# A hybrid encoder layer whose inputs also arrive transposed, with the norm weights applied in the operands' split and the tokens' factors applied to results

## The chip, the cores and the metric

The kernel runs on one core of a Trainium2 chip. A core has a matrix engine (TensorE, called PE in the profile; PEld is its weight load), a vector engine (VectorE, DVE), an engine for functions of one operand (ScalarE, ACT), a general one (GpSimd, POOL) and SyncE (SP), which here only issues DMAs. Each works through its own list of instructions in a fixed order, and waits at an instruction until what it needs has been written. The metric is device time in microseconds of one execution.

## The reference, cut to what matters

One layer over 1024 tokens of 1024 channels (x) and 256 tokens of a memory (mem). Both are normalised first, and everything before the attention is computed from the two normalised arrays:

```python
def rmsnorm(x, w):                      # each token by its own mean square, each channel by w
    return x * rsqrt(mean(x * x, axis=-1) + EPS) * w

mem_n = rmsnorm(mem, norm_mem_w)        # 256 x 1024
kv    = mem_n @ xkv_w                   # 256 x 2048, used later by the cross-attention

hn    = rmsnorm(x, norm_mix_w)          # 1024 x 1024
ca, cb, rq, rk, rv, rg = split(hn @ w_in)        # 512, 512, 256, 256, 512, 512 columns
u     = ca * sigmoid(cb)                # causal depthwise convolution, 31 taps, over u
y_conv = silu(layernorm(conv31(u) + conv_b))
q, k  = rotate(rq, positions), rotate(rk, positions)     # angles: position * inv_freq
y_ret = silu(rg) * groupnorm(retention(q, k, rv))        # 8 heads, in chunks
h     = x + concat(y_conv, y_ret) @ w_out
# then h += cross-attention to kv, h += squared-ReLU MLP, and a last rmsnorm
```

## The kernel before, in words

Large products are made from operands split in two: `hi` is the value rounded to the type fp32r, `lo` the rest. `mm3` issues three products, hi·hi (L128), hi·lo (L129) and lo·hi (L130). A split of what has been loaded is a copy on ACT (L110) and a subtraction on DVE (L111); `load` is a DMA (L120) and a split. Most of the memory on the chip is one pool of 39 slots of 4 KB per partition, given out first in, first out: a DMA into a slot waits until its last reader is done. A framework decides each engine's order of instructions when the program is built; on the chip the order is fixed.

The products need x and mem with channels on the partitions, and the inputs come with tokens there. So the kernel loads 128 tokens at a time (`fetch`, L180), squares and sums a row on ACT (L160), finds the reciprocal root on POOL (`rstd_of`, L142 and L143), multiplies by it and by the norm's weights, broadcast to all partitions (`row`, L148), on DVE (L162), transposes 128x128 blocks on PE against an identity (L170 for x: 64 of them; L203 for the memory: 16) and splits what comes out, from the accumulator memory, on ACT (L174) and DVE (L175, for the memory L208).

The program's first part goes in this order. The memory is prepared; `mem_project` c = 0 to 3 multiplies it by 256 columns of `xkv_w` each, ACT copies the result (L226) and a DMA stores it (`kvT_d`); between these, the eight tiles of x are prepared (`x_load`, `x_prep`). Then come a transpose of the convolution's parameters (L295, into `par`) and one of the positions (L321); DVE copies the latter to `pos_f` (L322). From `pos_f` POOL works out the rotary angles, reduced exactly to one turn, in some 70 small instructions (L328, L330, L333; "the angle chain"), and ACT takes cosine and sine (L379, L380) into `cos_t` and `sin_t`.

`conv_input(m)`, m = 0 to 3, makes 128 channels of u: four groups of 24 products of 512 columns (cb and ca for each half of the tokens), the sigmoid on ACT (L396), the product with ca on DVE (L397). Its weights are loaded one step ahead (L120, `raw`); the other four `mem_project` stand in the program between conv_input(0) and conv_input(1). The convolution is 124 steps on DVE (`conv_steps`, L433, 31 taps for each m; a tap's first one is L430), which the framework places where it thinks that DVE is free. Then V (copied by ACT) and g (Silu on ACT) are made for each tile of 128 tokens, and last the stage of the retention: for each tile a product with the q and k weights, `rotate` on DVE (L478, L483, L485, L488), `turn`, which transposes the rotated tile on PE (L497), and `retain`, with products of its own (L516, L532) and the update of a state on DVE. The weights of the output projection (`w_out`) are loaded while this stage runs, four after its tile 4 and four after tile 5. The cross-attention and the MLP follow.

Of the kernel before, what the change touches and what calls it, by code (L numbers as in the profile page):

```python
# [68 lines left out]
def encoder_layer(ctx: ExitStack, tc: tile.TileContext, x, mem, positions, norm_mix_w, w_in, conv_w, conv_b,  # L69
                  conv_ln_w, conv_ln_b, ret_gn_w, w_out, norm_xattn_w, norm_mem_w, xq_w, xkv_w, xo_w,  # L70
# [5 lines left out]
    memf = mem.rearrange("b s d -> (b s) d")  # L76
# [16 lines left out]
    def tbank():  # L93
        return bank("tp", 3)
# [19 lines left out]
    def load(w, k0, nk, c0, ncol, spare=False):  # L114

        if spare:
            raw = get([P, nk, ncol])
        else:
            raw = stage_tile([P, nk, ncol])
        sync.dma_start(raw[:], w[k0 * P:(k0 + nk) * P, c0:c0 + ncol].rearrange("(k p) c -> p k c", p=P))  # L120
        hi, lo = split(raw, [P, nk, ncol])
        if spare:
            put(raw)
        return hi, lo
# [7 lines left out]

    ident_if = keep.tile([P, C_DM], F32, name="ident_if")
    sync.dma_start(ident_if[:], consts[:, :C_DM])
    ident, invf = ident_if[:, :P], ident_if[:, C_IF:C_DM]
    mhalf = keep.tile([P, 32], F32, name="mhalf")
    vec.memset(mhalf[:], -0.5)
# [39 lines left out]

    def fetch(src):
        t = get([P, D])
        sync.dma_start(t[:], src)  # L180
        return t

    mems = [fetch(memf[t * P:(t + 1) * P, :]) for t in range(2)]
    mrow = row(norm_mem_w)
    mT_hi = [get([P, 2, 512], F32R) for _ in range(2)]
    mT_lo = [get([P, 2, 512], F32R) for _ in range(2)]

    def mem_view(tiles, k):

        return tiles[k // 4].t.rearrange("p a b -> p (a b)")[:, (k % 4) * M:(k % 4 + 1) * M]  # L190

    def mem_weights(c, spare=False):
        return [load(xkv_w, 4 * q, 4, 256 * c, 256, spare) for q in range(2)]

    mw = {0: mem_weights(0)}
    for t in range(2):
        xn = mems[t]
        rms_scaled(xn[:], mrow[:], xn[:])
        for q in range(2):
            tp = tbank()  # L200
            for kk in range(4):
                k = q * 4 + kk
                pe.transpose(tp[:, kk * P:(kk + 1) * P], xn[:, k * P:(k + 1) * P], ident)  # L203
            v = tp[:].rearrange("p (k c) -> p k c", k=4)
            h = mT_hi[q].t.rearrange("p a b -> p (a b)").rearrange("p (k m) -> p k m", k=4)[:, :, t * P:(t + 1) * P]
            l = mT_lo[q].t.rearrange("p a b -> p (a b)").rearrange("p (k m) -> p k m", k=4)[:, :, t * P:(t + 1) * P]
            act.copy(h, v)
            vec.tensor_tensor(out=l, in0=v, in1=f32(h), op=ALU.subtract)  # L208
        put(xn)
    put(mrow)  # L210
# [3 lines left out]
    def mem_project(c):  # L214
# [4 lines left out]
        for j in range(2):  # L219
            o = ps[:, j * M:(j + 1) * M]  # L220
            for k in range(NK):
                hi, lo = w[k // 4]
                lc = slice(j * P, (j + 1) * P)
                mm3(o, hi[:, k % 4, lc], lo[:, k % 4, lc], mem_view(mT_hi, k), mem_view(mT_lo, k),
                    k == 0, k == NK - 1)
        act.copy(st[:], ps[:].rearrange("p (j m) -> p j m", j=2))  # L226
# [5 lines left out]
    xT = [([get([P, 2, 512], F32R) for _ in range(4)], [get([P, 2, 512], F32R) for _ in range(4)]) for _ in range(2)]  # L232
    xs = {}

    def x_load(*ts):
        for t in ts:
            xs[t] = fetch(xf[t * P:(t + 1) * P, :])

    def x_prep(*ts):
        for t in ts:  # L240
            xn = xs.pop(t)
            rms_scaled(xn[:], xrow[:], xn[:])
# [981 lines left out]
```

## Time and profile before

| what | value |
|---|---|
| median of 3 runs | 1310.49 us (1307.62 to 1312.49) |
| the profiled execution's own time | 1311.58 us |
| its span in the trace | 1309.8 us |
| mean granted TensorE clock | 0.993 |
| busy: PE / DVE / ACT / POOL | 1279.6 / 862.3 / 548.4 / 95.7 us |
| the first 60 us: PE / DVE / ACT / POOL | 48.0 / 39.5 / 39.6 / 13.1 us |
| 60 to 120 us | 60.0 / 41.0 / 23.4 / 39.8 us |
| 120 to 260 us | 138.7 / 138.0 / 22.5 / 0.0 us |
| 260 to 420 us | 156.9 / 112.9 / 90.5 / 25.4 us |

The busy time of an engine is the time in which it has an instruction under way; times within the program are microseconds from the span's start. A row of the trace names the start, the duration, the engine, the line of the kernel, what is written and what is read, and in brackets how long the engine had stood idle before it and on whom it waited. A group's row gives the number of instructions, their busy time, the mean duration in ns, and the idle time just before them.

### The profile page before, as it was taken

To read this page: it belongs to the slowest core of one execution; us is meant where nothing else is said; L and a number is where in the kernel's file an instruction comes from. 1 tells how busy PE (TensorE), PEld (TensorE's weight loads), DVE (VectorE), ACT (ScalarE), POOL (GpSimd) and SP (SyncE) were. 2 spreads that over 40 slices of the span, in tenths; PEclk is the share of its full clock that TensorE was granted. 3 is DMA by queue.
4 is the path that set the end of the run, shared out by engine and by line. 5 is a ranking of instruction groups with operands and counts; after the bars stand their busy time and mean duration, and the time that the engine had idled before them with its cause. 6 is when DMAs were issued, how large, how long until landed. Compare 5 with 4: busy or idle time off the path is not lost.

```text
span 1309.8 us, 15796 instructions
## 1 busy us (share of the span) xinstructions
PE 1279.6 (98%) x6093; PEld 1066.4 (81%) x6093; DVE 862.3 (66%) x1090; ACT 548.4 (42%) x1015; POOL 95.7 (7%) x157
## 2 busy tenths in 40 slices
PE   6999999999999999999998999999999999999997
PEld 6898887877888888888877888888888888888886
DVE  6677999977756424574568655555564976577744
ACT  6533112155845323452236554444464344323422
POOL 3192000011211000000000000000000000000002
PEclk9999999999999999999998999999999999999999
DMA  9552103312142401232142443334469544444313
GB/s 340 167 154 89 32 17 97 113 41 89 35 143 93 130 4 41 90 112 72 58 145 81 177 161 145 119 123 177 161 240 400 198 159 152 141 149 159 106 65 129
DMA packets 82100, 166.99 MB, mean 127 GB/s; under 512 B 5310, under 2 KB 42310, under 8 KB 82025
## 3 DMA queue, kind: packets, MB, share of 16 engines
q1 hardware_dynamic: 82024, 165.98, 37.1%
q8 instruction: 48, 0.79, 0.2%
q14 instruction: 28, 0.22, 0.0%
HBM read 119.83 MB, written 46.14 MB: 127 GB/s over the span
## 4 chain that ended last, share of the span: by engine, by line
PE 78%; DVE 13%; POOL 3%; DMA 3%; issue 2%; ACT 1%; SPq 0%; POOLq 0%; ACTq 0%; DVEq 0%
PE mm L130 21%; PE mm L129 21%; PE mm L128 21%; DVE s L433 9%; PE tp L128 3%; PE tp L130 3%; PE tp L129 3%; DVE s L111 2%; POOL s L328 2%; PE mm L516 1%; POOL s L333 1%; PE mm L532 1%; ACT s L110 1%; DMA raw<-in_w_out_dram 1%; DMA s<-in_conv_w_dram 1%
## 5 line engine op out<-in xcount | busy, mean ns | idle before, releaser
L129 PE MATMUL mm<-s,s 128*128 128x512 f32 (+1 forms) x1298 | 494.3, 381 | 3.2 <-DVE s L111 1.7
L128 PE MATMUL mm<-s,s 128*128 128x512 f32 (+1 forms) x1272 | 485.0, 383 | 2.5 <-ACT s L856 1.0
L130 PE MATMUL mm<-s,s 128*128 128x512 f32 (+1 forms) x1222 | 462.0, 381 | 1.1 <-DVE s L111 1.1
L129 PEld LDWEIGHTS mm<-s,s 128*128 128x128 f32 x1298 | 245.3, 189 | 49.0 <-DVE s L111 2.5
L128 PEld LDWEIGHTS mm<-s,s 128*128 128x128 f32 x1272 | 240.4, 189 | 47.8 <-ACT s L856 1.3
L130 PEld LDWEIGHTS mm<-s,s 128*128 128x128 f32 x1222 | 230.9, 189 | 43.8 <-DVE s L111 1.7
L110 ACT CAST s<-s 128x1024 fp32r<-128x1024 f32 x101 | 104.8, 1051 | 143.6 <-DVE s L911 40.9
L433 DVE SCALAR_TENSOR_TENSOR s<-s,par,s 128x1009 f32<-128x1009 f32 (+25 forms) x120 | 146.1, 1276 | 0.5
L111 DVE TENSOR_TENSOR s<-s,s 128x1024 fp32r<-128x1024 f32 x81 | 98.3, 1224 | 57.0 <-ACT s L110 45.5
L111 DVE TENSOR_TENSOR s<-raw,s 128x1024 fp32r<-128x1024 f32 x64 | 78.8, 1237 | 55.1 <-ACT s L110 22.5
L110 ACT CAST s<-raw 128x1024 fp32r<-128x1024 f32 x66 | 69.3, 1055 | 93.2 <-PE mm L129 15.3
L142 POOL TENSOR_SCALAR tiny<-tiny 128x1 f32<-128x1 f32 (+1 forms) x50 | 18.4, 368 | 1177.2 <-ACT junk L160 921.1
L911 DVE TENSOR_TENSOR s<-s,s 128x1024 f32<-128x1024 f32 x38 | 46.0, 1223 | 7.3 <-DMA s<-in_mlp_down_w_dram 5.1
L129 PE MATMUL mm<-s,r 128*128 128x512 f32 x124 | 48.3, 390 | 0.0
L128 PE MATMUL tp<-s,s 128*128 128x512 f32 x120 | 46.8, 390 | 0.0
L110 ACT CAST s<-r 128x1024 fp32r<-128x1024 f32 x26 | 27.2, 1050 | 42.9 <-PE mm L129 13.5
L130 PE MATMUL tp<-s,s 128*128 128x512 f32 x114 | 44.2, 389 | 0.0
L162 DVE SCALAR_TENSOR_TENSOR s<-s,tiny,s 128x1024 f32<-128x1024 f32 x23 | 29.4, 1283 | 20.3 <-POOL tiny L143 12.8
L111 DVE TENSOR_TENSOR s<-r,s 128x1024 fp32r<-128x1024 f32 x22 | 26.9, 1225 | 21.4 <-ACT s L110 15.3
L130 PE MATMUL mm<-s,r 128*128 128x512 f32 x100 | 39.0, 390 | 0.0
L160 ACT ACTIVATE junk<-s 128x1024 f32<-128x1024 f32 x24 | 25.6, 1065 | 31.8 <-DVE s L1115 24.0
L130 PE MATMUL mm<-r,s 128*128 128x512 f32 x98 | 38.1, 389 | 0.0
(273 smaller groups left out, 1857.5 us busy)
## 6 DMA issues: line engine op xcount, KB each, us to landing
s<-in_mlp_down_w_dram SPq DMA_DIRECT2D x24, 512.0 KB, 3.8
s<-in_mlp_up_w_dram SPq DMA_DIRECT2D x23, 512.0 KB, 4.1
aS<-s SPq DMA_DIRECT2D x22, 512.0 KB, 8.5
raw<-in_w_in_dram SPq DMA_DIRECT2D x20, 512.0 KB, 4.2
s<-aS SPq DMA_DIRECT2D x20, 512.0 KB, 3.8
s<-a SPq DMA_DIRECT2D x19, 512.0 KB, 4.6
a<-s SPq DMA_DIRECT2D x18, 512.0 KB, 2.8
raw<-in_xkv_w_dram SPq DMA_DIRECT2D x16, 512.0 KB, 4.4
```

What stands on the lines that cost most here:

```text
L110: act.copy(hi[:], raw[:])
L111: vec.tensor_tensor(out=lo[:], in0=raw[:], in1=f32(hi[:]), op=ALU.subtract)
L128: pe.matmul(ps, lh, rh, start=first, stop=False, skip_group_check=goes_on)
L129: pe.matmul(ps, lh, rl, start=False, stop=False, skip_group_check=goes_on)
L130: pe.matmul(ps, ll, rh, start=False, stop=last, skip_group_check=goes_on)
L142: pool.tensor_scalar(out=v[:], in0=ss, scalar1=scale, scalar2=EPS, op0=ALU.mult, op1=ALU.add)
L160: act.activation(junk[:], src, AF.Square, accum_out=ss[:])
L162: vec.scalar_tensor_tensor(out=dst, in0=src, scalar=rs[:], in1=r, op0=ALU.mult, op1=ALU.mult)
L328: pool.tensor_scalar(out=o, in0=i, scalar1=a, scalar2=None, op0=op0)
L333: pool.tensor_tensor(out=o, in0=a, in1=b, op=op)
L433: vec.scalar_tensor_tensor(out=accs[m][:, s:], in0=us[m][:, :S - s], scalar=cw(m, k), in1=accs[m][:, s:], op0=ALU.mult, op1=ALU.add)
L911: vec.tensor_tensor(out=o[:], in0=a[:], in1=b[:], op=ALU.subtract)
```

## The change

The host passes three more arrays: x transposed (`x_t`), mem transposed (`mem_t`), and the weights of the two norms as columns (`norm_cols`). x itself is still passed, for the residual.

- The 80 transposes, the normalising instruction and the two broadcasts of weights are gone. A row of x_t has one channel on each partition and all tokens along it, so the norm's weight is one number per partition: `scaled_split` makes hi on ACT as a copy with a scale, and lo on DVE as raw · w - hi in one instruction. The operands hold x · w, without the tokens' factors.
- The tokens' factors, 1 / rms, are worked out beside this. ACT squares each raw tile; for x, POOL adds the eight squares up in seven instructions of 128x1024 (L277 of the new kernel); for the memory DVE reduces them. `token_factors` sums over the partitions with products of two columns against ones, ACT copies the sums, POOL finds the reciprocal roots. This gives `x_rs`, tokens on the partitions. `spread` makes the row form: DVE multiplies the identity by a column of factors, PE multiplies ones by that (L224), ACT copies it out: `x_rb` and `mem_rs`, the same on every partition.
- The factors enter where results are read. In `conv_input` DVE multiplies cb by `x_rb` (L440), the sigmoid works in place (L441), DVE multiplies by `x_rb` (L442) and then by ca (L443, as before). In `mem_project` the copy on ACT becomes a multiplication on DVE (L254). V's copy and g's Silu take the factor as the scale of the same ACT instruction. For q and k POOL multiplies `cos_t` and `sin_t` by the factors, two instructions.
- mem_project(3) and the loads around it stand in another order, `mw[4]` is loaded before conv_input(0)'s weights, x's operands are freed only after tile 5 of the retention, and all eight loads of `w_out` stand there.

```diff
+    def scaled_split(hi, lo, raw, w):
+        act.activation(hi, raw, AF.Copy, scale=w)
+        vec.scalar_tensor_tensor(out=lo, in0=raw, scalar=w, in1=f32(hi), op0=ALU.mult, op1=ALU.subtract)
...
+    def token_factors(sums, nt, out):
+
+        ps = tbank()
+        for t in range(nt):
+            for z, q in enumerate(sums):
+                pe.matmul(ps[:, 2 * t:2 * t + 2], q[:, t * P:(t + 1) * P], ones[:, :2], start=z == 0,
+                          stop=z == len(sums) - 1)
+        ss = tiny(nt)
+        act.copy(ss[:], ps[:, :2 * nt].rearrange("p (t z) -> p t z", z=2)[:, :, 0])
+        r = rstd_of(ss[:], 1, 1.0 / D, nt)
+        if out is not None:
+            vec.tensor_copy(out, r[:])
+        return r
+
+    def spread(r, t, ps, scratch):
+
+        vec.tensor_scalar(out=scratch, in0=ident, scalar1=r[:, t:t + 1], scalar2=None, op0=ALU.mult)
+        pe.matmul(ps, ones, scratch, start=True, stop=True)
...
-        act.copy(st[:], ps[:].rearrange("p (j m) -> p j m", j=2))
+        vec.tensor_tensor(out=st[:], in0=ps[:].rearrange("p (j m) -> p j m", j=2),
+                          in1=mem_rs.unsqueeze(1).to_broadcast([P, 2, M]), op=ALU.mult)
...
-    def x_prep(*ts):
-        for t in ts:
-            xn = xs.pop(t)
-            rms_scaled(xn[:], xrow[:], xn[:])
-            transposed(xn, *xT[t // 4], (t % 4) * P)
-            put(xn)
...
+    def x_prep(*ks):
+        for k in ks:
+            raw = xs.pop(k)
+            xT[k] = hi, lo = get([P, S], F32R), get([P, S], F32R)
+            scaled_split(hi[:], lo[:], raw[:], mix_w[:, k:k + 1])
+            sq = get([P, S])
+            act.activation(sq[:], raw[:], AF.Square)
+            if not xss:
+                xss.append(sq)
+            else:
+                pool.tensor_tensor(out=xss[0][:], in0=xss[0][:], in1=sq[:], op=ALU.add)
+                put(sq)
+            put(raw)
...
+    x_rb = get([P, S])
+    token_factors([xss[0][:]], NT, x_rs)
+    for half in range(2):
+        tp = tbank()
+        for i in range(4):
+            spread(x_rs, half * 4 + i, tp[:, i * P:(i + 1) * P], work[:, 5 + i % 3, :])
+        act.copy(x_rb[:, half * 512:(half + 1) * 512], tp[:])
+    put(xss.pop())
...
+            vec.tensor_tensor(out=uh, in0=pb[:], in1=x_rb[:, hh], op=ALU.mult)
+            act.activation(uh, uh, AF.Sigmoid)
+            vec.tensor_tensor(out=uh, in0=uh, in1=x_rb[:, hh], op=ALU.mult)
             vec.tensor_tensor(out=uh, in0=pa[:], in1=uh, op=ALU.mult)
...
-    nxt = conv_weights(0)
-    mw[4] = mem_weights(4)
...
-        if t == 4:
-            wo += [load(w_out, k, 1, 0, D) for k in range(4)]
         if t == 5:
             for w in wqk:
                 put(*w)
-            wo += [load(w_out, k, 1, 0, D) for k in range(4, NK)]
+            for k in range(NK):
+                put(*xT[k])
+            wo += [load(w_out, k, 1, 0, D) for k in range(NK)]
```

How the change moves instructions is seen in the order that each engine is given. In a row stand the line, the operation, what is written and read (tp and mm are accumulators, s_ a slot of the pool, ident_if the identity) and the size.

PE, around the transpose of the positions (tp<-ident_if,s 128x8), before; mm_780 and mm_781 are the accumulators of conv_input(0)'s second half, mm_845 that of a mem_project:

```order
L128 MATMUL mm_781<-s_20_150,s_61_705 128x512
L128 MATMUL mm_780<-s_20_150,s_63_711 128x512
L128 MATMUL mm_845<-s_4_83,s_65_717 128x256
L129 MATMUL mm_845<-s_6_85,s_65_717 128x256
L130 MATMUL mm_845<-s_4_83,s_66_718 128x256
L129 MATMUL mm_781<-s_24_154,s_61_705 128x512
L295 MATMUL tp_630<-ident_if,s_53_623 128x35 x4
L321 MATMUL tp_643<-ident_if,s_55_639 128x8
L130 MATMUL mm_781<-s_20_150,s_62_706 128x512
L128 MATMUL mm_781<-s_20_150,s_61_705 128x512
```

and after, where mm_656 is an accumulator of conv_input(0)'s second half, and mm_723 that of mem_project(4):

```order
L124 MATMUL mm_656<-s_61_454,s_77_597 128x512
L125 MATMUL mm_656<-s_60_453,s_78_598 128x512
L123 MATMUL mm_656<-s_63_460,s_77_597 128x512
L224 MATMUL tp_494<-s_11_114 128x128 x3
L335 MATMUL tp_514<-ident_if,s_67_507 128x35 x4
L361 MATMUL tp_527<-ident_if,s_69_523 128x8
L124 MATMUL mm_656<-s_64_461,s_77_597 128x512
L125 MATMUL mm_656<-s_63_460,s_78_598 128x512
L123 MATMUL mm_723<-s_3_79,s_53_387 128x256
L124 MATMUL mm_723<-s_5_81,s_53_387 128x256
L125 MATMUL mm_723<-s_3_79,s_54_388 128x256
```

Before, the transpose stands in the midst of conv_input(0)'s second half, 45 products ahead of its end; now two products are left there, behind the products that spread the factors (L224).

POOL, from the first instruction that reads data, before (L142 and L143 are the reciprocal roots for a tile of tokens):

```order
L142 TENSOR_SCALAR tiny_101<-tiny_99 128x1
L143 TENSOR_TENSOR tiny_102<-tiny_101,mhalf 128x1
L142 TENSOR_SCALAR tiny_122<-tiny_120 128x1
L143 TENSOR_TENSOR tiny_123<-tiny_122,mhalf 128x1
L142 TENSOR_SCALAR tiny_230<-tiny_228 128x1
L143 TENSOR_TENSOR tiny_231<-tiny_230,mhalf 128x1
```

and after:

```order
L277 TENSOR_TENSOR s_27_224<-s_27_224,s_30_230 128x1024
L138 TENSOR_SCALAR tiny_129<-tiny_127 128x2
L277 TENSOR_TENSOR s_27_224<-s_27_224,s_40_305 128x1024
L139 TENSOR_TENSOR tiny_130<-tiny_129,misc 128x2
L277 TENSOR_TENSOR s_27_224<-s_27_224,s_43_312 128x1024
L277 TENSOR_TENSOR s_27_224<-s_27_224,s_49_375 128x1024
L277 TENSOR_TENSOR s_27_224<-s_27_224,s_52_382 128x1024
L277 TENSOR_TENSOR s_27_224<-s_27_224,s_62_457 128x1024
L277 TENSOR_TENSOR s_27_224<-s_27_224,s_65_464 128x1024
L138 TENSOR_SCALAR tiny_479<-tiny_477 128x8
L139 TENSOR_TENSOR tiny_480<-tiny_479,misc 128x8
L373 TENSOR_TENSOR s_70_530<-pos_f,ident_if 128x128
```

Between the two reciprocal roots for the memory and the one for x now stand the additions, and the angle chain (from L373) follows behind them.

ACT, around the sine (sin_t), before (L226 copies a result of the memory, L396 is conv_input(1)'s sigmoid):

```order
L110 CAST s_90_1090<-raw_1088 128x1024
L110 CAST s_92_1096<-raw_1094 128x1024
L380 ACT_TABLE_LOAD
L380 ACTIVATE sin_t<-s_56_646 128x8x16
L226 COPY s_89_1036<-mm_1037 128x512
L110 CAST s_95_1207<-raw_1205 128x1024
L379 ACTIVATE cos_t<-s_56_646 128x128
L110 CAST s_97_1213<-raw_1211 128x1024
L110 CAST s_101_1431<-raw_1429 128x1024
L396 ACT_TABLE_LOAD
L396 ACTIVATE s_94_1100<-mm_1102 128x512
```

and after (L441 is the sigmoid of conv_input(1), L109 a copy for a split):

```order
L109 CAST s_102_974<-raw_972 128x1024
L109 CAST s_105_1089<-raw_1087 128x1024
L109 CAST s_107_1095<-raw_1093 128x1024
L420 ACT_TABLE_LOAD
L420 ACTIVATE sin_t<-s_70_530 128x8x16
L441 ACT_TABLE_LOAD
L441 ACTIVATE s_104_978<-s_104_978 128x512
L419 ACT_TABLE_LOAD
L419 ACTIVATE cos_t<-s_70_530 128x128
```

Between the sine and the first sigmoid of conv_input(1) stood three copies of weights, a result of the memory and the cosine; now that sigmoid comes right behind it, and the cosine behind the sigmoid.

DVE, at the first rotation (rot, L478), before (L433 is a convolution step, L488 the last instruction of a rotation):

```order
L433 SCALAR_TENSOR_TENSOR s_60_702<-s_100_1322,par,s_60_702 128x997
L433 SCALAR_TENSOR_TENSOR s_60_702<-s_100_1322,par,s_60_702 128x996
L478 TENSOR_TENSOR rot_1969<-mm_1944,cos_t 128x512
L483 TENSOR_TENSOR rb_1970<-mm_1944,sin_t 128x16x16 x2
L433 SCALAR_TENSOR_TENSOR s_60_702<-s_100_1322,par,s_60_702 128x995
L485 TENSOR_TENSOR rot_1969<-rot_1969,rb_1970 128x512
L478 TENSOR_TENSOR rot_2002<-mm_1977,cos_t 128x512
L433 SCALAR_TENSOR_TENSOR s_60_702<-s_100_1322,par,s_60_702 128x994
L488 TENSOR_TENSOR kz_1975<-rot_1969,rconst 128x256
```

and after (L479 is a convolution step, L524 and L529 a rotation's first instructions, L564 the retention's masked scores):

```order
L479 SCALAR_TENSOR_TENSOR s_73_587<-s_109_1099,par,s_73_587 128x996
L479 SCALAR_TENSOR_TENSOR s_74_588<-s_110_1208,par,s_74_588 128x1002
L524 TENSOR_TENSOR rot_1859<-mm_1834,cos_t 128x512
L529 TENSOR_TENSOR rb_1860<-mm_1834,sin_t 128x16x16 x2
L479 SCALAR_TENSOR_TENSOR s_73_587<-s_109_1099,par,s_73_587 128x995
L524 TENSOR_TENSOR rot_1892<-mm_1867,cos_t 128x512
L479 SCALAR_TENSOR_TENSOR s_74_588<-s_110_1208,par,s_74_588 128x1001
L531 TENSOR_TENSOR rot_1859<-rot_1859,rb_1860 128x512
L479 SCALAR_TENSOR_TENSOR s_73_587<-s_109_1099,par,s_73_587 128x994
L479 SCALAR_TENSOR_TENSOR s_74_588<-s_110_1208,par,s_74_588 128x1000
L524 TENSOR_TENSOR rot_1940<-mm_1915,cos_t 128x512
L534 TENSOR_TENSOR kz_1865<-rot_1859,rconst 128x256
```

Before, two steps of the convolution are left at the first rotation; now the steps of two channels' groups (s_73 and s_74) stand between the instructions of the rotations, ten from here on.

168 lines of the change are left out of this document (87 added, 81 removed).

## The prediction

> **What bounds the kernel now.** I read the page's first part, the waits of TensorE, the busy times by stretch, and then the order of time on DVE, ACT and POOL up to 270 us, where the change works.
>
> ```profile
> PE 1279.6 (98%) x6093; PEld 1066.4 (81%) x6093; DVE 862.3 (66%) x1090; ACT 548.4 (42%) x1015; POOL 95.7 (7%) x157
> PE tp L203 <- DVE s L162: 9.5, 1, 9.5
> PE tp L497 <- DVE rot L485: 2.5, 1, 2.5
> 100.00:120.00 20.00, 20.00 (x90) 16.57 (x89) 11.06 (x10) 9.37 (x12) 5.50 (x12) 1.00 0.38 118
> 180.00:200.00 20.00, 20.00 (x90) 16.57 (x89) 20.00 (x18) 3.41 (x5) 0.00 (x0) 1.00 0.00 1
> 260.00:280.00 20.00, 17.49 (x81) 13.55 (x80) 14.98 (x28) 7.82 (x36) 0.13 (x1) 0.91 0.06 24
> ```
>
> In the stretches the columns are length, PE, PEld, DVE, ACT, POOL, granted clock, DMA share, GB/s. Over the program PE is the bound, and one would price the change by PE work alone. But from 120 us on DVE is as full as PE (20.00 of 20 at 180), and at 267 us PE waits 2.51 us for the first rotated tiles. Up to there the two run neck and neck: whatever PE saves earlier is worth nothing unless DVE also arrives earlier, and whatever DVE loses is paid in full.
>
> So the question is what sets DVE's arrival at 260.88, the first rotation:
>
> ```profile
> 62.75 0.40 POOL L333 TENSOR_TENSOR s<-pos_f,ident_if 128x128 f32<-128x128 f32 x1 [23.56 <-DVE pos_f L322]
> 105.07 0.56 POOL L330 TENSOR_SCALAR s<-s 128x128 f32<-128x128 f32 x2
> 105.40 0.31 ACT L380 ACTIVATE sin_t<-s 128x128 f32<-128x128 f32 x1 [10.36 <-POOL s L330]
> 108.83 2.36 DVE L111 TENSOR_TENSOR s<-raw,s 128x1024 fp32r<-128x1024 f32 x2 [9.50 <-DMA kvT_d<-s]
> 260.88 0.60 DVE rot L478
> 267.45 1.11 PE L497 MATMUL tp<-ident_if,rot 128*128 128x128 f32 x4 [2.51 <-DVE rot L485]
> L433 DVE SCALAR_TENSOR_TENSOR s<-s,par,s 128x1000 f32<-128x1000 f32 (+25 forms) x107 | 128.8, 1269 | 0.3
> L111 DVE TENSOR_TENSOR s<-raw,s 128x1024 fp32r<-128x1024 f32 x15 | 18.2, 1226 | 11.3 <-DMA kvT_d<-s 9.5 <-ACT s L110 1.8
> L397 DVE TENSOR_TENSOR s<-mm,s 128x512 f32<-128x512 f32 x6 | 4.1, 686 | 0.0
> L430 DVE TENSOR_SCALAR s<-s,par 128x1024 f32<-128x1024 f32 x3 | 2.4, 810 | 0.0
> ```
>
> POOL's angle chain starts when `pos_f` is there (62.75) and takes 42.6 us. ACT stands in order behind it for 10.36 us (the sine), what ACT owes is late, and DVE stands still for 9.50 us. It resumes at 108.83 and then works without a pause for 152.05 us up to 260.88. The last four rows, of 108 to 262 us, are that work: 128.8 + 18.2 + 4.1 + 2.4 = 153.5. A later `pos_f` is therefore a later rotation, microsecond for microsecond.
>
> **The change, part by part: what PE saves.**
>
> ```profile
> L170 PE MATMUL tp<-ident_if,s 128*128 128x128 f32 x64 | 8.6, 272 | 0.0
> L203 PE MATMUL tp<-ident_if,s 128*128 128x128 f32 x16 | 3.9, 428 | 9.8 <-DVE s L162 9.5 <-DVE s L208 0.2
> 313.88 1.72 PE mm L516 x4
> 54.53 0.87 PE tp L170 x8
> L170 PEld LDWEIGHTS tp<-ident_if,s 128*128 128x128 f32 x64 | 7.3, 140 | 0.4
> ```
>
> 64 transposes of x go, at 0.87 / 8 = 0.109 us: 7.0 us; 16 of the memory, 3.9. Added are 10 f32 products of 128 columns (`spread`): an f32 product of 512 columns is two records, four of them take 1.72, so 0.86 for 512 and 0.215 for 128: 2.2 us. The 12 `token_factors` products have two columns; no row shows that. Between 0.109 (a transpose's issue) and two f32 weight loads at 140 ns with 0.08 beside them, 0.36: I take 0.25, 3.0 us, 2.0 of it for x. Net PE work falls by 5.7 us, and PE no longer waits 9.5 us for normalised rows. By PE alone the answer would be faster.
>
> **Where conv_input(0) can start.** Its third product (L130, now L125) needs the low half of the first conv weights, the last of the front's splits: 46.95 before.
>
> ```profile
> 24.08 0.28 PE L128 MATMUL mm<-s,s 128*128 128x256 f32 x1
> 24.20 0.28 PE L129 MATMUL mm<-s,s 128*128 128x256 f32 x1
> 46.95 0.50 PE mm L130
> 60.90 0.22 PE L321 MATMUL tp<-ident_if,s 8*128 8x8 f32 x1
> 94.05 0.40 PE L128 MATMUL mm<-s,s 128*128 128x512 f32 x1
> L175 DVE TENSOR_TENSOR s<-tp,s 128x256 fp32r<-128x256 f32 x32 | 12.3, 418 | 3.2 <-ACT s L174 3.0
> L162 DVE SCALAR_TENSOR_TENSOR s<-s,tiny,s 128x1024 f32<-128x1024 f32 x10 | 12.7, 1282 | 10.2 <-DMA s<-in_norm_mem_w_dram 7.3 <-POOL tiny L143 2.9
> 31.95 2.04 ACT L110 CAST s<-raw 128x1024 fp32r<-128x1024 f32 x2
> 46.75 0.65 ACT L174 CAST s<-tp 128x256 fp32r<-128x256 f32 x2
> 5.12 1.06 ACT L160 ACTIVATE junk<-s 128x1024 f32<-128x1024 f32 x1 [3.12 <-DMA s<-in_mem_dram]
> 64.50 0.46 POOL L333 TENSOR_TENSOR s<-s 128x128 f32<-128x128 f32 x1
> 6.35 0.19 POOL L142 TENSOR_SCALAR tiny<-tiny 128x1 f32<-128x1 f32 x1 [4.19 <-ACT junk L160]
> 79.78 0.54 POOL L328 TENSOR_SCALAR s<-s 128x128 f32<-128x128 f32 x1
> 71.72 1.39 POOL L328 TENSOR_SCALAR s<-s 128x128 f32<-128x128 f32 x1
> 82.52 1.48 DVE L111 TENSOR_TENSOR s<-raw,s 128x1024 fp32r<-128x1024 f32 x1
> ```
>
> ACT: up to the cast of those weights the new order has about 26 passes of 1024 (8 scales of x, 7 squares of x, 2 of the memory, 9 casts of weights up to L109 on `raw_589`), issued every 1.0 us (two in 2.04), 8 scales of 256 at 0.3 (two in 0.65), and small copies: 34 to 35 us. The first data come at 5.1 as before, so 40 is the earliest. The DMAs hide under this; two rows of weights broadcast to 128 partitions (1 MB) fall away.
>
> DVE: 8 scaled splits of 256 at 0.33 (2.6), 2 reductions (2.4), 11 weight splits of 1.2 (13.5), 8 scaled splits of x at 1.28 (10.2), 4 results of the memory moved over from ACT at 0.68 (2.7), small ones 0.6: 32.0 us. The work DVE loses in L175 and L162 comes back in these forms. Alone, with the pauses that it has now, that ends near 43.
>
> POOL: seven new adds of 128x1024. No row shows one. L333 takes 0.46 for 128 columns, of which 0.19 is an instruction with nothing in it (L142): 8 x 0.27 + 0.19 = 2.35; ends 1.2 (DVE's time for the shape, L111) and 3.7 (8 x 0.46). They are not free. With DVE busy an angle step of 0.54 takes 1.39 (71.72), as if it waited for one whole DVE instruction, and L111 on DVE takes 1.48 instead of 1.23. If each holds the other off, six adds before the weights' split (14.1) and 32.0 us lie in a row from 5.2: 51.3. SP stands behind them too: positions and, behind them, the conv weights are issued only after POOL's fifth add has freed a slot.
>
> So the third product comes between 43 and 51.3. I take 48, a little nearer the upper end because the rows show the holding off on both sides: +1.0 against 46.95.
>
> The page "SBUF — State Buffer" of the Trainium skill (section "Who interferes with whom") says that a DVE instruction with two SBUF inputs and a GpSimd instruction that reads SBUF exclude each other for the whole instruction. The 1.39 and 1.48 above agree; by that rule the sum would use 51.3 and come out 3.3 us higher, without it 43 and 5 us lower. The "GPSIMD Engine Reference" (section "Performance versus the Vector engine") gives 4497 ns for an add of 2048, which makes an estimate of 2.25 us here.
>
> **From there to `pos_f`.** Before, the transpose of the positions stood 13.95 us behind that third product (60.90 - 46.95). Now PE's order puts it behind 92 of conv_input(0)'s remaining products at 0.222 (90 in 20.00 us, the stretch at 180): 20.4; eight sums for x, 2.0; seven `spread`, 1.5; and the parameters' transposes, 0.5: 24.4. The wait inside (the sums need POOL's seventh add) is covered by 20 products, 4.4 us; without that cover its 2.35 would be added. So `pos_f` is 10.4 + 1.0 = 11.4 us later, near 74.2.
>
> **From `pos_f` to the end.** The angle chain is the same; its two new products come behind the sine.
>
> ```profile
> 111.80 1.28 ACT L396 ACT_TABLE_LOAD   x1
> 113.09 0.60 ACT L396 ACTIVATE s<-mm 128x512 f32<-128x512 f32 x1
> ```
>
> ACT is again stopped by it, and now its sine stands in front of conv_input(1)'s first sigmoid, which DVE needs for L442: the sine's 0.31, a table load and a sigmoid, 1.28 + 0.60, together 2.2 us after the sine's start, where before 3.4 passed (105.40 to 108.83): -1.2. Then DVE's work to the first rotation: 102 convolution steps at 1.204 (128.8 / 107), 12 splits at 1.213, 17 instructions of 512 at 0.683 (three in each half of a conv_input for one, less the one done already), 3 starts at 0.8: 151.4 against 153.5, so -2.1. But only because steps are left over: behind the first rotation ten convolution steps now stand between it and the state update, where two stood. Eight steps are 9.6 us; DVE has 5.0 us free in 260 to 280, so 4.6 remain (ends 0 and 9.6).
>
> Sum: 11.4 - 1.2 - 2.1 + 4.6 = +12.7. PE's savings do not enter: PE arrives before DVE. What follows (V and g read with the token's factor in the same instruction, all eight output weights fetched after the sixth step, freed slots) I cost at nothing: the same instruction with a scale, and loads under some 70 us of products; if those are late it costs a split, 2.4 us. The profiled execution took 1311.58, 1.1 over the median of 1310.49; on the median 1323.2.
>
> **Rivals.** *No change:* the adds do not hold DVE off (third product at 43, -5.0), the small sums hide under their neighbours (-1), and DVE's pauses take in all the left-over steps (-4.6): 12.7 - 10.6 = +2.1, 1312.6. For it speaks that PE and DVE wait for each other in that stretch; against it 1.39 and 1.48. *Faster:* the front runs at ACT's limit (third product at 40.5) and the angle chain runs at POOL's own pace. Its 45 or so steps of 0.46 to 0.54 and their gaps would be 28 us alone instead of 42.6, since DVE may have less ready to do beside it. Then PE sets the time: 40.5 + 24.4 + 0.4 + 0.2 + 192 products of the memory 0.12 apart (23.0) = 88.5 against 94.05, and behind it 170.9 us as before (264.94 - 94.05) to the first rotated transpose: 259.4 against 267.45, -8.0, 1302.5. It decides where the chain ends by about 95; against it, DVE has 28 us of work ready beside the chain, as before. *Slower still:* everything at its upper end: 51.3, 0.36 for each small sum, no free DVE: 12.7 + 3.3 + 0.9 + 5.0 = +21.9, 1332.4; that is the upper part of my own case.
>
> **Numbers.** About 0.5% (6.5 us) is what a measurement of this kernel can tell from no change. My case 0.61, from 1314 to 1332, nearly all of it slower; no change 0.22; faster 0.17. The range takes in the faster case at its price and goes up to the upper bounds: 1302 to 1333.
>
> **What would show it.** Right: the first product before 9 us, but the third of conv_input(0) near 48; POOL with seven adds above 2 us each and DVE instructions stretched beside them; `pos_f`'s transpose near 73; the sine on ACT near 117 after a wait for POOL; DVE idle some 10 us before it; PE's wait at the first rotated tiles and behind it larger than 2.5 us, in all by ten or more. Wrong: a sine at or before 106, or a PE that does not wait between 255 and 290.

## The result, and the profile after

The changed kernel takes 1327.05 us, median of 5 runs (1324.75 to 1330.56), against 1308.7 us (1307.62 to 1312.49) for the kernel before, 5 runs: 1.0138 of the time, 95% interval 1.0114 to 1.0162, 18 us slower. The profiled execution is the fastest of its five (1324.75 us, span 1322.9), and that of before is near the slow end of its own, so the two traces lie only 13.1 us apart. Now and then an execution of one of these kernels takes far longer (2159.72 and 2613.24 us among the experiments); such runs are left out of the medians, and the second of them is the only profiled execution of the kernel with both repairs.

From the page, the chain of waits and the order of time on PE, POOL, ACT and DVE, the rows of the changed kernel that answer to those shown of before. L125 is the third product of `mm3`, L361 the transpose of the positions, L373 the first step of the angle chain, L420 the sine, L442 the multiplication behind the sigmoid, L524 a rotation and L543 its transpose:

```profile
PE 1279.6 (97%) x6057; PEld 1064.3 (80%) x6057; DVE 880.6 (67%) x1097; ACT 550.1 (42%) x984; POOL 111.8 (8%) x151
10.21 0.58 PE L123 MATMUL mm<-s,s 128*128 128x256 f32 x1 [10.21 <-ACT s L109]
50.98 0.50 PE L123 MATMUL mm<-s,s 128*128 128x512 f32 x1 [1.08 <-ACT s L109]
52.70 0.50 PE L125 MATMUL mm<-s,s 128*128 128x512 f32 x1 [0.98 <-DVE s L110]
77.66 0.23 PE L361 MATMUL tp<-ident_if,s 8*128 8x8 f32 x1
78.17 0.40 POOL L373 TENSOR_TENSOR s<-pos_f,ident_if 128x128 f32<-128x128 f32 x1 [16.73 <-DVE pos_f L362]
120.83 0.31 ACT L420 ACTIVATE sin_t<-s 128x128 f32<-128x128 f32 x1 [11.48 <-POOL s L370]
123.12 0.69 DVE L442 TENSOR_TENSOR s<-s,s 128x512 f32<-128x512 f32 x1 [11.84 <-ACT s L441]
270.76 0.60 DVE rot L524
275.61 0.66 PE L543 MATMUL tp<-ident_if,rot 128*128 128x128 f32 x4
```

Each step stands where the prediction looked for it, and later: the third product at 52.70 (46.95 before), the positions at 77.66 (60.90), the sine at 120.83 after a wait of 11.48 us for POOL (105.40 after 10.36), DVE's return at 123.12 after 11.84 us of idle time (108.83 after 9.50), the first rotation at 270.76 (260.88). The memory needs no transposes any more, yet PE starts no sooner: its first product comes at 10.21, and before its first transpose came at 9.54.

In the front, the first 60 us, the groups of DVE and POOL instructions (count, busy time, mean ns) show why the third product is late. First the changed kernel, on POOL and DVE:

```profile
L277 POOL TENSOR_TENSOR s<-s,s 128x1024 f32<-128x1024 f32 x7 | 19.6, 2796 | 30.2 <-ACT tiny L215 16.4 <-ACT s L273 13.7
L110 DVE TENSOR_TENSOR s<-raw,s 128x1024 fp32r<-128x1024 f32 x12 | 21.0, 1760 | 5.4 <-ACT s L109 5.4
L182 DVE SCALAR_TENSOR_TENSOR s<-s,misc,s 128x1024 fp32r<-128x1024 f32 x8 | 14.2, 1810 | 0.0
```

and the kernel before, DVE:

```profile
L111 DVE TENSOR_TENSOR s<-raw,s 128x1024 fp32r<-128x1024 f32 x12 | 14.6, 1220 | 4.4 <-DMA kvT_d<-s 3.7 <-ACT s L110 0.6
```

The same twelve splits of weights take 1760 ns each instead of 1220 while POOL adds.

How this reaches PE is seen in the rows ahead of conv_input(0) in the changed kernel: an addition, the split beside it, the wait of SyncE's DMA queue (SPq) between 41.6 and 46, the load that the queue then issues, and the copy on ACT that needs what is loaded.

```profile
41.66 2.77 POOL L277 TENSOR_TENSOR s<-s,s 128x1024 f32<-128x1024 f32 x1 [5.27 <-ACT s L273]
42.12 3.40 DVE L110 TENSOR_TENSOR s<-raw,s 128x1024 fp32r<-128x1024 f32 x1
SPq L115 <- DVE s L110: 3.5, 1, 3.5
45.55 0.39 SPq L115 DMA_DIRECT2D raw<-in_w_in_dram  x1
49.88 1.04 ACT L109 CAST s<-raw 128x1024 fp32r<-128x1024 f32 x1 [3.46 <-DMA raw<-in_w_in_dram]
```

The addition ends at 44.43, and the split, which began beside it, at 45.52, 1.09 us later. Only then is the load of conv_input(0)'s first weights issued, at 45.55 (at 38.95 in the run below with the additions on DVE, and at 29.48 before, where the loads stand in another order). ACT waits for it, and PE's first product of conv_input(0) comes 1.10 us after ACT's copy began.

Last, what PE waits for from 100 us on. The changed kernel between 100 and 276, and the stretch in which this wait lies:

```profile
PE mm L124 <- DVE s L110: 3.5, 1, 3.5
```

```profile
200.00:220.00 20.00, 16.54 (x69) 13.32 (x68) 20.00 (x18) 3.95 (x5) 0.00 (x0) 0.95 0.04 6
```

and three rows of the waits of its whole span, which are at the rotations:

```profile
PE mm L575 <- DVE rb L529: 1.8, 1, 1.8
PE mm L578 <- DVE pm L564: 1.6, 1, 1.6
PE mm L562 <- ACT qb L549: 1.5, 1, 1.5
```

The 3.5 us lie between 200 and 220, at the weights of g, where before 1.3 were lost. The 2.51 us between the transposes of the first and the second rotated tile are gone; instead 4.9 us of waits stand behind the first transpose, where another 0.6 stood. Of the 4.9, 1.5 are a wait for ACT.

So the first rotated transpose comes 11.3 us later than before (275.61 against 264.35), but the rows don't say by whose fault: PE itself began conv_input(0) 5.3 us late, and DVE came back late too. That is what the experiments had to take apart.

### The profile page after: what moved, and what is told of

It is laid out like the page before. It is cut to its first block, busy times and chain, and to the rows that moved or that the text cites. A ratio compares the mean times of both kernels' runs of the same rounds, so it can differ in the third digit from the quotient of the medians.

```text
span 1322.9 us, 15684 instructions
## 1 busy us (share of the span) xinstructions
PE 1279.6 (97%) x6057; PEld 1064.3 (80%) x6057; DVE 880.6 (67%) x1097; ACT 550.1 (42%) x984; POOL 111.8 (8%) x151
## 4 chain that ended last, share of the span: by engine, by line
PE 78%; DVE 13%; POOL 3%; issue 2%; ACT 2%; DMA 2%; POOLq 0%; SPq 0%; DVEq 0%; ACTq 0%
PE mm L124 21%; PE mm L125 21%; PE mm L123 21%; DVE s L479 7%; PE tp L123 3%; PE tp L124 3%; PE tp L125 3%; DVE s L110 2%; POOL s L368 2%; POOL s L373 1%; DVE s L182 1%; DMA raw<-in_xkv_w_dram 1%; PE mm L578 1%; DMA raw<-in_xo_w_dram 1%; ACT s L109 0%
## 5 line engine op out<-in xcount | busy, mean ns | idle before, releaser
L123 PE MATMUL mm<-s,s 128*128 128x512 f32 (+1 forms) x1272 | 486.9, 385 | 13.2 <-ACT s L109 11.3
L125 PE MATMUL mm<-s,s 128*128 128x512 f32 (+1 forms) x1222 | 462.9, 381 | 8.4 <-DVE s L110 8.4
L125 PEld LDWEIGHTS mm<-s,s 128*128 128x128 f32 x1222 | 232.2, 190 | 52.3 <-DVE s L110 9.7
L109 ACT CAST s<-s 128x1024 fp32r<-128x1024 f32 x101 | 104.8, 1051 | 143.1 <-DVE s L956 38.8
L479 DVE SCALAR_TENSOR_TENSOR s<-s,par,s 128x999 f32<-128x999 f32 (+26 forms) x120 | 146.1, 1275 | 0.1
L138 POOL TENSOR_SCALAR tiny<-tiny 128x1 f32<-128x1 f32 (+2 forms) x42 | 14.1, 336 | 1149.0 <-ACT junk L156 893.8
L110 DVE TENSOR_TENSOR s<-raw,s 128x1024 fp32r<-128x1024 f32 x64 | 85.7, 1346 | 33.3 <-ACT s L109 17.9
L109 ACT CAST s<-raw 128x1024 fp32r<-128x1024 f32 x66 | 68.5, 1049 | 81.6 <-DMA raw<-in_w_in_dram 23.6
L956 DVE TENSOR_TENSOR s<-s,s 128x1024 f32<-128x1024 f32 x38 | 45.9, 1220 | 7.2 <-DMA s<-in_mlp_down_w_dram 5.1
L124 PE MATMUL mm<-s,r 128*128 128x512 f32 x124 | 48.4, 390 | 0.0
L109 ACT CAST s<-r 128x1024 fp32r<-128x1024 f32 x26 | 27.2, 1051 | 42.6 <-PE mm L124 13.6
L125 PE MATMUL tp<-s,s 128*128 128x512 f32 x114 | 44.2, 389 | 0.0
L110 DVE TENSOR_TENSOR s<-r,s 128x1024 fp32r<-128x1024 f32 x22 | 26.8, 1222 | 21.5 <-ACT s L109 15.4
L125 PE MATMUL mm<-s,r 128*128 128x512 f32 x100 | 38.9, 389 | 0.0
L125 PE MATMUL mm<-r,s 128*128 128x512 f32 x98 | 38.0, 389 | 0.0
L123 PE MATMUL mm<-s,r 128*128 128x512 f32 x96 | 37.2, 391 | 0.0
L1056 DVE TENSOR_TENSOR s<-s,mm 128x512 f32<-128x512 f32 x24 | 16.4, 684 | 31.1 <-PE mm L125 31.1
```

Source lines behind the costliest of these rows:

```text
L109: act.copy(hi[:], raw[:])
L110: vec.tensor_tensor(out=lo[:], in0=raw[:], in1=f32(hi[:]), op=ALU.subtract)
L123: pe.matmul(ps, lh, rh, start=first, stop=False, skip_group_check=goes_on)
L124: pe.matmul(ps, lh, rl, start=False, stop=False, skip_group_check=goes_on)
L125: pe.matmul(ps, ll, rh, start=False, stop=last, skip_group_check=goes_on)
L138: pool.tensor_scalar(out=v[:], in0=ss, scalar1=scale, scalar2=EPS, op0=ALU.mult, op1=ALU.add)
```

## The experiments

Each is named by what it changes. Ratios are to the kernel before, run beside it, with 95% intervals. Gains on the changed kernel are given against its 1327.05, which was measured in another round: the kernel before took 1308.7 us beside it, and 1310.2, 1310.5 and 1309.9 beside the experiments, so by the ratios these gains come out 1 to 2 us larger.

**The angle chain first.** The theory of the prediction was that the late chain delays DVE and DVE the rotation. The chain is moved ahead of x's preparation:

```diff
+    pos_f = ra.tile([P, NT], F32, name="pos_f")
+    sync.dma_start(pos_i[:], positions.rearrange("b (t p) -> (b t) p", p=P))
...
+    ts(thc, thc, lim, ALU.min, -lim, ALU.max)
+    ts(ang, ang, lim, ALU.min, -lim, ALU.max)
     mw[1] = mem_weights(1)
     mem_project(0)
```

> The changed kernel with one thing moved: the load and transpose of the positions and the whole angle chain stand ahead of the preparation of x, so the sine is ready long before ACT comes to it. The additions on POOL, the factors and the multiplications by them stay. Theory (the late angle chain stops ACT and with it DVE): DVE's idle time of 11.84 us before 123 disappears; the next bound is PE, whose third product of conv_input(0) at 52.70 plus the 217.4 us that lie between it and the first rotated transpose before gives 270 against 275.6, and the steps of the convolution left over at the rotations (4.8 us) go too: 8 to 11 us less, 1316 to 1319. Rival 'work' (DVE's additional multiplications and left-over steps cost the time, wherever the sine stands): within 2 us of 1327. Rival 'front' (all that counts is that conv_input(0) starts 5.8 us later on PE): within 2 us of 1327, or later still if the angle chain holds off DVE's splits in the front.

Measured: 1330.66 us (1.0157, 1.0142 to 1.0172), no gain at all. The same in the kernel before:

> The kernel before, with its positions and angle chain moved ahead of the preparation of x in the same way. Theory: its 9.50 us of DVE idle time disappear, and PE's wait of 2.51 us at the first rotated tiles with the 1.3 us that it waits between 200 and 220; PE is then the bound: 3 to 4 us less than 1308.7, about 1305. Rivals 'work' and 'front': no change, or some us more, since the chain now runs beside the front's splits on DVE.

Measured: 1319.36 us (1.0076, 1.0057 to 1.0094), 9 us lost where 3 to 4 were to be won. Order of time in the changed kernel with the chain first; the first product of conv_input(0), and the first rotated transpose:

```profile
59.99 0.80 PE L123 MATMUL mm<-s,s 128*128 128x512 f32 x1 [13.58 <-ACT s L109]
282.82 0.60 PE L543 MATMUL tp<-ident_if,rot 128*128 128x128 f32 x4
```

and in the kernel before with the chain first:

```profile
54.85 0.50 PE L128 MATMUL mm<-s,s 128*128 128x512 f32 x1
```

The chain's instructions on POOL now run in the front, and conv_input(0) starts at 59.99 instead of 50.98, at 54.85 instead of 45.69 before. In the changed kernel ACT's copy of the first weights now waits 3.45 us for an addition, which stands among the chain's instructions on POOL:

```profile
58.89 1.04 ACT L109 CAST s<-raw 128x1024 fp32r<-128x1024 f32 x1 [3.45 <-POOL s L277]
```

All that was gained behind was lost ahead: DVE's stop at the sigmoid is gone in the changed kernel (1.3 us at most, instead of 11.84), but PE starts 9.0 us later and the first rotated transpose comes 7.2 us later. Both kernels lost where both were to win, the kernel before as much as its start moved (9.2). The theory by which DVE's stop carries everything had its first miss here.

**Without the additions.** The seven instructions on POOL are taken away:

```diff
-                pool.tensor_tensor(out=xss[0][:], in0=xss[0][:], in1=sq[:], op=ALU.add)
```

> The changed kernel without the seven additions on POOL: the factors of x come from the first eighth of the channels' squares alone, so the sums are left out. All else stays, though the framework moves the transpose of the positions ahead again (51 of conv_input(0)'s products earlier or more). Theory with the holding off between POOL and DVE: DVE's splits in the front run at 1.2 us instead of up to 3.4, the third product of conv_input(0) comes at 44 to 46 instead of 52.70, the positions some 20 us earlier, the sine before 105: 12 to 18 us less, 1309 to 1315. Without the holding off, the third product stays near 52 (it waited for the weights' DMA) and only the positions' place helps: 1318 to 1321. Rival 'work': 1325 or more.

Measured: 1306.0 us (0.9968, 0.9957 to 0.9978), better than any of the theories gave. The first product of conv_input(0):

```profile
44.82 0.50 PE L123 MATMUL mm<-s,s 128*128 128x512 f32 x1 [1.02 <-ACT s L109]
```

It is the additions, then, that make the front late, and the DMA of the weights is late through them: the load is issued at 38.25 here, and at 45.55 with them. But the framework had moved the transpose of the positions ahead too, so the front and the stop at the sine went together.

**Row sums on ACT, chain first.**

```diff
+        xr = fetch(xf[t * P:(t + 1) * P, :])
+        act.activation(junk[:], xr[:], AF.Square, accum_out=ssx[:, t:t + 1])
```

> The changed kernel with the angle chain early as in the first run, and the sums for x's factors taken in another way: ACT squares the rows of x as passed before and adds them up in the same instruction, as many ACT passes as now, so POOL's seven additions and the eight small products that sum over partitions are gone; x is loaded once more (4 MB). Theory: both delays gone, third product of conv_input(0) at 45 to 48, no stop for the sine: 18 to 22 us less, 1305 to 1309. If the loads of the front are what sets its pace, the 4 MB more, 12 us at 350 GB/s, come in front of the convolution's weights: 1315 to 1325.

Measured: 1319.49 us (1.0075, 1.006 to 1.009), as the rival had it: conv_input(0) starts at 55.17. It has two causes in one, the chain on POOL and 4 MB more of loads. The trace shows the loads at work: ACT waits 3.65 us for rows of x, and five of its squares stand in front of the copy that PE waits for (54.09). How much is the chain's was not tried apart.

**The sine held back.** Now the stop alone is taken away. Cosine and sine get a bias of zeros made from a later result, so that the framework has to place them behind it; the front stays as it is:

```diff
+    zc = tiny()
+    act.activation(zc[:], us[2][:, :1], AF.Copy, scale=0.0)
+    act.activation(cos_t[:], thc.rearrange(...), AF.Sin, bias=zc[:])
```

> The changed kernel with cosine and sine held back on ACT: they take a bias of zeros that is made from conv_input(2)'s result, so they stand behind four of the later sigmoids, and ACT no longer stops for the angle chain. The front, the chain on POOL and the order of PE are the same. What the first four runs left: the time followed the start of conv_input(0) on PE, and the early angle chain cost the front more than it could give. Theory 'two delays' (front 5.3 us, sums and spreads on PE 2.5 us, DVE's stop for the rest): DVE's idle time of 11.84 us goes, PE's stall at the weights of g (5.2 us here, 1.8 before) goes and the 3.4 us of left-over steps at the retention too, 5 to 8 us less: 1319 to 1322. Theory of the prediction (DVE's arrival passes on in full): 11 to 12 us less, 1315. Rival 'front alone': no change, 1326 to 1328.

Measured: 1319.89 us (1.007, 1.0044 to 1.0096; three runs), 7.2 us less. The interval is too wide to tell 7 us from the 11 to 12 of the prediction's theory by the time alone; the trace below does. And in the kernel before:

> The kernel before with cosine and sine held back on ACT in the same way; its front is untouched. Theory 'two delays' and that of the prediction: the 9.50 us of DVE idle time go, with them PE's 2.51 us at the first rotated tiles and 1.3 us between 200 and 220: 3 to 4 us less than before, about 1305. Rival 'front alone': no change.

Measured: 1305.38 us (0.9962, 0.9948 to 0.9977), 5 us less than before: the fastest of the kernels here that compute the whole layer. Rows of the changed kernel with the sine held back: the start of conv_input(0), PE between 200 and 220 us (columns as in the prediction), and the first rotated transpose:

```profile
50.85 0.50 PE L123 MATMUL mm<-s,s 128*128 128x512 f32 x1 [0.98 <-ACT s L109]
200.00:220.00 20.00, 20.00 (x90) 16.57 (x89) 20.00 (x18) 7.30 (x8) 0.00 (x0) 1.00 0.34 97
270.25 0.60 PE L547 MATMUL tp<-ident_if,rot 128*128 128x128 f32 x4
```

The start is the same to 0.13 us. The wait at the weights of g is gone (90 products in the stretch, where the changed kernel had 69), and PE reaches the rotations 5.4 us sooner. The first rotation's row on DVE now shows it waiting for PE:

```profile
264.17 0.69 DVE L528 TENSOR_TENSOR rot<-mm,cos_t 128x512 f32<-128x512 f32 x1 [1.20 <-PE mm L125]
```

So DVE has been brought forward until PE is the bound, and 5.9 us of the 11.3 remain (270.25 against 264.35): those are PE's own, 5.2 of them its later start (50.85 against 45.69).

**The additions on DVE.**

```diff
-                pool.tensor_tensor(out=xss[0][:], in0=xss[0][:], in1=sq[:], op=ALU.add)
+                vec.tensor_tensor(out=xss[0][:], in0=xss[0][:], in1=sq[:], op=ALU.add)
```

> The changed kernel with the seven additions on DVE instead of POOL, all else in the same place on PE (the first sigmoid of conv_input(1) now comes ahead of the sine). DVE has 7 x 1.22 = 8.6 us more work in the front, and nothing on POOL to be held off by. If POOL and DVE hold each other off for whole instructions (19 us of additions on POOL beside DVE splits of up to 3.4 us), DVE's front ends earlier although it has more to do: third product of conv_input(0) at 46 to 49, 4 to 8 us less, 1319 to 1323. If they only share a little, it comes at 55 or later, and the time is 1327 to 1331.

Measured: 1317.17 us (1.0054, 1.0038 to 1.0069), 9.9 us less. Its groups on DVE in the first 60 us, and the third product:

```profile
L110 DVE TENSOR_TENSOR s<-raw,s 128x1024 fp32r<-128x1024 f32 x12 | 14.4, 1219 | 2.5 <-ACT s L109 2.5
L182 DVE SCALAR_TENSOR_TENSOR s<-s,misc,s 128x1024 fp32r<-128x1024 f32 x8 | 10.1, 1274 | 0.0
L277 DVE TENSOR_TENSOR s<-s,s 128x1024 f32<-128x1024 f32 x7 | 8.5, 1216 | 0.3 <-ACT s L273 0.3
```

```profile
48.19 0.50 PE L125 MATMUL mm<-s,s 128*128 128x512 f32 x1 [0.53 <-DVE s L110]
```

This is the plainest reading of the case. DVE does more and is done sooner: the splits go back from 1760 and 1810 ns to 1219 and 1274, 10.7 us in all (6.6 + 4.1), for 8.5 us of additions. On POOL the same additions took 19.6. The third product comes 4.5 us earlier. The gain in time is larger than that and larger than expected. DVE's stop ends earlier as well (the sine at 119.40 instead of 120.83), PE's wait at the weights of g falls from 3.5 to 2.2 us, and the first rotated transpose comes at 269.90, 5.7 us earlier. The traces lie 8.1 us apart (spans of 1314.8 and 1322.9), so 2.4 of that lie behind the first rotated transpose.

**The sums on PE, the sine held back.**

```diff
+            for t in range(NT):
+                pe.matmul(xss[0][:, 2 * t:2 * t + 2], sq[:, t * P:(t + 1) * P], ones[:, :2], ...)
```

> The changed kernel with the sums for x's factors made on PE (64 products of two columns, 0.21 us each, 13.4 us in all, accumulated as the squares come), no additions on POOL, and the sine held back as in the other run. PE stands idle 20.5 us in the first 60, where these products find room. Theory 'two delays': both go; third product of conv_input(0) at 46 to 49, no stop on ACT, 9 to 13 us less: 1314 to 1318. If PE's front has no room after all, the start of conv_input(0) comes at 55 or later: 1322 and more.

Measured: 1323.82 us (1.0105, 1.0088 to 1.0121), the worse of the two outcomes: conv_input(0) starts at 61.00. The products for the sums come in the midst of the memory's, and what hangs on these comes later: ACT's copy of the first weights of conv_input(0) begins at 59.90, after waiting 11.29 us for the store of a result of the memory. PE's clock, too, was lower in this front (last section), so the two are not told apart.

**Both repairs.** Additions on DVE and the sine held back:

> The changed kernel with both single repairs: the additions on DVE and the sine held back. Theory 'two delays': the front as in the run with the additions on DVE (third product of conv_input(0) near 48.2), and no stop on ACT (DVE's idle time of 10.7 us and PE's stalls at the weights of g gone): 4 to 6 us under that run's 1317, so 1311 to 1313; not below the kernel before, since the front is still 1.2 us later and the sums and spreads put 2.5 us on PE. If the two repairs give the same microseconds, it stays at 1316 to 1318.

Measured: 1311.66 us (1.0011, 1.0001 to 1.0021), as expected. Of the 18 us, 15.4 are gone, and each repair keeps nearly its own size: 1317.17 - 1311.66 = 5.5 for the sine, 1319.89 - 1311.66 = 8.2 for the additions.

**The memory's part alone, the sine held back.**

> The memory's part of the change alone (transposed memory, its weights in the split, its factors on the results, results read by DVE), x as before the change, and the sine held back; to be compared with the kernel before with the sine held back, 1305.4. PE loses 16 transposes (3.9 us) and the 9.5 us that it waited for normalised rows; DVE and ACT have about the same to do. Theory (the front is set by ACT's and DVE's splits, not by PE): conv_input(0) starts within 1.5 us of 45.3 and the time is 1304 to 1307. If PE's transposes and wait did set the front, it starts 3 us or more earlier: 1300 to 1302.

Measured: 1307.96 us (0.9987, 0.9977 to 0.9998), 1 us above the range expected and 2.6 over the kernel before with the sine held back. The start of conv_input(0):

```profile
46.89 0.50 PE L123 MATMUL mm<-s,s 128*128 128x512 f32 x1 [0.20 <-ACT s L109]
```

It is 1.6 us later than the 45.32 of that kernel. PE's 16 transposes and its wait of 9.5 us are gone, and nothing is gained.

**Without x's factor on u.** From the kernel with both repairs, 16 multiplications on DVE are taken away:

```diff
-            vec.tensor_tensor(out=uh, in0=pb[:], in1=x_rb[:, hh], op=ALU.mult)
-            act.activation(uh, uh, AF.Sigmoid)
-            vec.tensor_tensor(out=uh, in0=uh, in1=x_rb[:, hh], op=ALU.mult)
+            act.activation(uh, pb[:], AF.Sigmoid)
```

> The kernel with both repairs, without the 16 multiplications by x's factors in conv_input (u is computed from unnormalised values, so its factor is left out; the sigmoid reads the accumulator directly). It takes 16 x 0.6 = 9.6 us from DVE. Rival 'work' (DVE's additional multiplications cost their time): 8 to 10 us less than the kernel with both repairs beside it. Theory 'two delays': with the stop gone DVE is no longer what PE waits for, but for a few us at the weights and the retention: 0 to 3 us less.

Measured: 1310.43 us (1.0, 0.9989 to 1.0012), 1.2 us less than the kernel with both repairs. The rival "work" falls: once DVE isn't stopped, 9.6 us of its work more or less hardly show.

## Why the prediction was right, and where it was not

The time (1323 forecast, 1327 measured), the sign and the places came out. The sum of +12.7 stands against 18 between the medians and 13.1 between the traces, and in part it is luck: the first rotation was forecast 8.1 us later and came 9.9 later, with the front 4.7 us worse than forecast and DVE's work behind the stop 2.3 us better; behind the first rotation 4.6 were forecast, and 3.2 measured. Point by point:

- **The front** was mis-sized. The third product was put at 48, with 51.3 as the upper bound; it came at 52.70. The additions took 2.80 us each instead of 2.35, and the splits beside them 0.54 us more each, twenty times over, where the upper bound only set POOL's six additions and DVE's work in a row. The 2.35 was right for an addition by itself (2.34 us each for most of them in the changed kernel with the chain first); what was too small is what the two add to each other. What carried it, the holding off, is shown: with the additions on DVE the splits go back. It reached PE by a way that the prediction had only in part: the load of the first weights waited for a split of DVE that an addition had drawn out to 3.40 us, not for the slot that an addition frees. The sign "first product before 9 us" did not appear (10.21). The Trainium skill's page "SBUF — State Buffer" (section "Who interferes with whom") gives such an exclusion; the trace agrees with it in this case (1219 ns alone, 1760 beside POOL, and the split of 42.12 that ends 1.09 us after the addition). By the estimate from the Trainium skill's "GPSIMD Engine Reference" (section "Performance versus the Vector engine"), 2.25 us for an addition, the sum would have been no better: 2.80 was measured, with DVE busy.
- **From the third product to the positions** 24.4 us were forecast, 25.0 measured (77.66 - 52.70).
- **The sine and DVE's return.** The stop was forecast near 117, and came at 120.83, the front's miss passed on. DVE's work to the first rotation took 147.6 us (270.76 - 123.12) instead of 151.4; before it took 152.05.
- **The steps left over** were put at 4.6 us; PE waited 4.9 us behind the first rotated transpose. That the two are alike is luck in part: 1.5 us of the 4.9 are a wait for ACT, which stands in the variants without the stop too, and from the first rotated transpose to the end the changed kernel takes only 1.8 us longer (1322.9 - 275.61 against 1309.8 - 264.35). The prediction's "first rotated transpose" at 267.45 is the second tile's; the first stands at 264.35, where PE did not wait.
- **The step that failed** is the sentence that PE's savings don't enter because PE arrives before DVE, and with it "a later `pos_f` is a later rotation, microsecond for microsecond". PE was late in its own right: it started conv_input(0) 5.3 us later, and the sums and spreads lie on its path. With DVE's stop taken away, 7.2 of the 18 us came back (5.5 once the additions stand on DVE), not 11 to 12, and 5.9 us stayed at the first rotated transpose, with DVE waiting for PE. The forecast was near since both paths were late by much the same and the sum counted the longer one; had the stop been cheap, it would have missed the 10 us of the front. The prediction's own sign for this, PE's waits behind the first rotated tiles growing by ten or more, did not appear: they grew by 1.8 (4.9 against 2.51 and 0.6).
- **The rivals.** "Faster" needed the chain to end by 95 with the front at ACT's limit. Where the additions are left out, the chain ended in time (the sine at 83.67), the front came nearer to that limit without reaching it (third product at 46.08, not 40.5), and the time was 1306.0, not 1302.5.
- **PE's fewer transposes** were rightly put at nothing as far as the memory goes: its part alone removes 16 of them with their wait, and is not faster. The 64 of x were not tried apart.

What stays open: 6.3 us between the changed kernel with both repairs and the kernel before with the sine held back (1311.66, 1305.38). The memory's part has 2.6 of them; for the rest, the eight sums and seven spreads on PE and a start still about 1 us late (third product at 48.19 with the additions on DVE, at 47.80 without x's factor on u, against 46.95) are likely, but were not tried one by one; nor was the changed order of the loads. What the additions on DVE gain behind the first rotated transpose (2.4 us between the traces) has no cause shown either.

## What to carry to other kernels

Ask of every instruction that is moved to a free engine whom it holds off there: seven additions that POOL did in its idle time cost DVE more (10.7 us) than DVE needs for doing them itself (8.5), and a split drawn out in this way kept back the next load of weights and with it PE. Where two engines run neck and neck, a sum over one path is not enough; work out both arrivals, and see which is left when the other is repaired. And look for an instruction that stands early in an engine's order only because it is expected to be ready: holding the sine back behind later sigmoids, in the unchanged kernel, was worth 5 us by itself.

## What the runs showed that was not expected

The angle chain is not free in the front. Moved ahead it makes conv_input(0) start 9 us later in both kernels, about as much as the stop that it avoids; of the places tried the best is where it was, with its reader moved. In four of the variants PE's granted clock in the first 60 us was below 1, 0.89 to 0.91 (the chain first in both kernels, the row sums, the sums on PE), in which products of 512 columns at the start of conv_input(0) took about 0.80 us instead of 0.50 (in the kernel before with the chain first, from the third one on); it was 1.00 in the kernel before and in the changed one, and 0.97 without the additions, with the additions on DVE and without x's factor on u. The row of the stretch, for the changed kernel with the chain first:

```profile
0.00:60.00 60.00, 31.12 (x206) 29.63 (x206) 36.58 (x38) 33.98 (x40) 38.51 (x37) 0.90 0.70 232
```

In this kernel the low clock stands at the wait before conv_input(0) and behind it (0.57 between 50 and 60, 0.58 between 60 and 70, after 13.58 us without a product); with the sums on PE it was 0.82 to 0.84 from 30 to 70, where PE had no such wait. What set the clock was not tried. It belongs to the losses of these variants (from the start of conv_input(0) to the first rotated transpose the changed kernel with the chain first takes 222.8 us, with the sine held back 219.4), and not to those of the two kernels compared.
